# Both FFN products as seven block products for eight, in two phases, with the blocks of hid passed through DRAM

## The chip, the cores and the metric

One core of a Trainium2 chip runs the kernel in one launch. The metric is device time in microseconds. Before the change it is 3207.47 us, the median of three runs (3206.49 to 3208.62). Five engines work side by side, each through its own instructions in order: TensorE (PE), VectorE (DVE), ScalarE (ACT), GpSimd (POOL) and SyncE (SP), which here issues nearly all transfers between DRAM and the on-chip memory (SBUF). Matrix products land in a second on-chip memory, PSUM.

## The reference

The same encoder layer is applied to two batches (prompt and sample), each of 1024 rows of 1024 numbers: an input projection, two kinds of attention, a gated output projection, a layer norm, and then the feed-forward network (FFN) that the change is about. In `encoder_layer`:

```
merged = sigmoid(ga + b_gate[0]) * ya + sigmoid(gb + b_gate[1]) * yb
x = layer_norm(DEEPNORM_ALPHA * x + merged @ w_out, ln1_g, ln1_b)
hid = square(relu(x @ w_ff1 + b_ff1))          # 1024 x 4096
x = layer_norm(DEEPNORM_ALPHA * x + hid @ w_ff2 + b_ff2, ln2_g, ln2_b)
```

All of it is float32. To multiply at that accuracy, the kernel splits every operand into a high and a low part in the rounded type `fp32r`, and each product takes three matmuls: high by high, low by high, high by low (`mm3`).

## The kernel before, in words

The two batches run one after the other. In each, after attention, the output projection (`pso`, 32 sums of 24 matmuls) gives rows of `acc`; each is normalised (`layer_norm`), transposed and split into `x1T` (`transposes`), and gets its residual and bias in place (L729). High parts are casts on ScalarE; low parts are subtractions, which all go through the helper at L103, on VectorE or GpSimd.

The FFN runs over 32 slices of 128 columns of hid, two at a time (the last four together). For a slice, `wunit` (L178) loads w1's 128 columns in two tiles of 256 KB, casts them (`whi`, L189) and subtracts (`wlo`); 48 matmuls `pmm` give 1024 rows of hid in two halves; ScalarE applies bias and relu (L754), GpSimd squares (L755), ScalarE casts (L756) and VectorE subtracts, so that `hh` and `hl` stay in SBUF. A row block of w2 is loaded (512 KB, `w2r`) and split (`w2h`, `w2l`). After two slices, 16 sums `psf` of 12 matmuls each follow, and VectorE adds each to `acc` (L773). Per batch these are 1536 and 1536 matmuls. At the end each row of `acc` is normalised again and written out.

The program's order is not written out by hand: all work is emitted to a scheduler that simulates a timeline and orders the instructions of each engine. Semaphores make an engine wait for what it reads and for buffers that must come free; SP issues its transfers in order, each behind those ahead of it.

Of the kernel before, what the change touches and what calls it, by code (L numbers as in the profile page):

```python
# [9 lines left out]
F32 = mybir.dt.float32  # L10
# [71 lines left out]
def encoder_kernel(ctx, tc, xs, w_in, b_gate, w_a, w_b, w_out, rpb, ln1_g, ln1_b, w1, b1, w2, b2,  # L82
# [22 lines left out]
    def mm3(out, ah, al, bh, bl, start, stop):  # L105
        nc.tensor.matmul(out, ah, bh, start=start, stop=False)  # L106
        nc.tensor.matmul(out, al, bh, start=False, stop=False)  # L107
        nc.tensor.matmul(out, ah, bl, start=False, stop=stop)  # L108
# [15 lines left out]
    gd = [dram.tile([2, KT, P, T], F32, name=f"gd{b}") for b in range(len(xs))]  # L124
    prd = dram.tile([8, PR, PC], F32, name="prd")
# [43 lines left out]
    wup = ctx.enter_context(tc.tile_pool(name="wu", bufs=2, reuse_waits="tile"))  # L169
    wrw = ctx.enter_context(tc.tile_pool(name="wraw", bufs=3, reuse_waits="tile"))  # L170
    sm = ctx.enter_context(tc.tile_pool(name="small", bufs=8, reuse_waits="tile"))
    pmm = ctx.enter_context(tc.tile_pool(name="pmm", bufs=2, space=PSUM, reuse_waits="tile"))
# [37 lines left out]
    def layer_norm(z, g, bb, last=0, lnt=None):  # L210

        mv = sm.tile([P, 2], F32, name="mv", tag="mv")
        if last == 1:

            junk = lnt.tile([P, D], F32, name="junk", tag="x")
# [7 lines left out]
        else:  # L223
            st = sm.tile([P, 2, 6], F32, name="bst", tag="bst")
            for j in range(2):
                nc.vector.bn_stats(st[:, j], z[:, j * 512:(j + 1) * 512])
# [21 lines left out]
    for b, x in enumerate(xs):  # L248
        rop = pool("rope", side="right")
        rope = rop.tile([P, 2, T], F32, name="rope")  # L250
        maska = rop.tile([P, 512], F32, name="maska")
# [5 lines left out]
        vp = pool("v")  # L257
        vrp = pool("vr", 4)
        vtp = pool("vt", 2)
# [430 lines left out]
        abp.release()  # L690


        accp = pool("acc", side="right")
        acc = accp.tile([P, 8, D], F32, name="acc")
        lnp = pool("ln1", side="right")
        g1, bb1, b2t = bcast(lnp, ln1_g, "g1"), bcast(lnp, ln1_b, "bb1"), bcast(lnp, b2, "b2t")
        x1T = bigT()
        pso = pool("ps_o", 4, space=PSUM)
        pst = pool("ps_t2", 2, space=PSUM)
        for h in range(2):  # L700
            for nh in range(2):
                wo = []
                for k in range(KT):
# [4 lines left out]
                    nc.scalar.copy(wh, raw)  # L708
                    sub(nc.gpsimd, wl, raw, f(wh))
                    wo.append((wh, wl))  # L710
                pss = [pso.tile([P, 512], F32, name="pso", tag="pso") for _ in range(4)]
                order = [(k, i) for k in range(KT) for i in range(4)]
                if nh == 1:
                    order.sort(key=lambda o: o[1])
                for k, i in order:
                    cs = slice(i * P, (i + 1) * P)
                    mm3(pss[i], mT[h][0][:, k, cs], mT[h][1][:, k, cs], *wo[k], k == 0, k == KT - 1)
                for i in range(4):
                    it = 4 * h + i
                    xt = xp.tile([P, D], F32, name="xt", tag="x")  # L720
                    ns = slice(nh * 512, (nh + 1) * 512)
                    nc.sync.dma_start(xt[:, ns], x[it * P:(it + 1) * P, ns])
                    nc.vector.scalar_tensor_tensor(acc[:, it, ns], in0=xt[:, ns], scalar=ALPHA, in1=pss[i],
                                                   op0=ALU.mult, op1=ALU.add)
            for i in range(4):
                it = 4 * h + i
                layer_norm(acc[:, it], g1, bb1)
                transposes(acc[:, it], pst, x1T[h][0], x1T[h][1], i * P)
                nc.vector.scalar_tensor_tensor(acc[:, it], in0=acc[:, it], scalar=ALPHA, in1=b2t, op0=ALU.mult, op1=ALU.add)  # L729
        pst.release()  # L730
        pso.release()
        lnp.release()
        wop.release()


        hidp = pool("hid", 4)
        w2p = pool("w2", 4)
        w2r = pool("w2r", 2)
        tmp = pool("ffn_t", 2)
        psf = pool("ps_f", 6, space=PSUM)  # L740
        nft = FF // P
        for c in [range(i, i + 2) for i in range(0, nft - 4, 2)] + [range(nft - 4, nft)]:
            hid, w2t = [], []
            for ft in c:
                fs = slice(ft * P, (ft + 1) * P)
                wu = wunit([w1[:, fs]])
                hh = hidp.tile([P, T], F32R, name="hh", tag="hh")
                hl = hidp.tile([P, T], F32R, name="hl", tag="hl")
                for h in range(2):
                    hs = slice(512 * h, 512 * (h + 1))  # L750
# [75 lines left out]
```

## Time and profile before

| | us |
|---|---|
| median of the runs | 3207.47 |
| profiled execution | 3202.68 |
| its span, first to last instruction | 3201.0 |
| TensorE busy | 3072.3 |
| VectorE busy | 1426.0 |
| GpSimd busy | 1299.0 |
| ScalarE busy | 1143.7 |

The span is the time between the first and the last instruction of one profiled execution; the runs are timed without a profile. The FFN of the first batch lies at about 911 to 1611 us in it, that of the second at about 2490 to 3188. A matmul's recorded duration overlaps with that of the next, so the distance between starts is what counts. [...]

### The profile page before, as it was taken

The page shows a single profiled execution, that of the slowest core. Times are in us where ns is not written, and L with a number is a line of the kernel's source. Part 1 is how long each engine was busy: PE and PEld are TensorE (multiplying, and loading weights), DVE is VectorE, ACT ScalarE, POOL GpSimd, SP SyncE. Part 2 cuts the span into 40 slices and gives each one's busy share as a digit, 9 for nine tenths or more (in the row PEclk, how much of TensorE's full clock was granted, in tenths as well). Part 3 has the DMA queues.
Part 4 walks back from the last instruction along what each step waited for, and adds up shares of the span by engine and source line. Part 5 has one row for each costly group of instructions (what it writes and reads, how often), then busy time and mean ns, then how long its engine had stood idle before and what let it go on. Part 6 is the DMA issues. An engine that isn't in the chain of part 4 may idle for free. (4 is left out here: it accounts for less than half of the span.)

```text
span 3201.0 us, 39935 instructions
## 1 busy us (share of the span) xinstructions
PE 3072.3 (96%) x14732; PEld 2567.3 (80%) x14732; DVE 1426.0 (45%) x3052; ACT 1143.7 (36%) x2222; POOL 1299.0 (41%) x959
## 2 busy tenths in 40 slices
PE   8889898999999999999989989999999999999998
PEld 7778687887778888888888877778878788888886
DVE  1156556744553333333331665666446433333334
ACT  3155464654222221122331655555532321222223
POOL 3565543214643333333441647242165433333333
PEclk9999998999999999999999999999999999999999
DMA  8732324445431111111163222244454211111111
GB/s 225 254 102 71 98 63 135 124 155 164 145 96 53 53 47 53 47 40 53 61 214 106 73 66 86 87 126 142 169 163 132 73 53 46 42 52 53 50 47 53
DMA packets 306267, 309.78 MB, mean 97 GB/s; under 512 B 33992, under 2 KB 263184, under 8 KB 305816
## 3 DMA queue, kind: packets, MB, share of 16 engines
q1 hardware_dynamic: 279576, 268.95, 27.8%
q10 hardware_dynamic: 26496, 38.28, 3.3%
q8 instruction: 116, 1.90, 0.2%
q14 instruction: 79, 0.65, 0.1%
HBM read 246.02 MB, written 62.09 MB: 96 GB/s over the span
## 5 line engine op out<-in xcount | busy, mean ns | idle before, releaser
L106 PE MATMUL pmm<-bh,whi 128*128 128x512 f32 x2176 | 860.3, 395 | 17.9 <-ACT r L415 17.4
L108 PE MATMUL pmm<-bl,whi 128*128 128x512 f32 x2176 | 857.1, 394 | 0.0
L107 PE MATMUL pmm<-bh,wlo 128*128 128x512 f32 x2176 | 856.6, 394 | 0.0
L103 POOL TENSOR_TENSOR wlo<-wraw,whi 128x512 fp32r<-128x512 f32 (+1 forms) x304 | 417.2, 1389 | 518.0 <-ACT whi L189 462.8
L106 PEld LDWEIGHTS pmm<-bh,whi 128*128 128x128 f32 x2176 | 411.8, 189 | 99.3 <-ACT r L415 18.3
L108 PEld LDWEIGHTS pmm<-bl,whi 128*128 128x128 f32 x2176 | 411.4, 189 | 81.9 <-DVE bl L103 0.4
L107 PEld LDWEIGHTS pmm<-bh,wlo 128*128 128x128 f32 x2176 | 411.8, 189 | 78.9
L773 DVE TENSOR_TENSOR acc<-acc,psf 128x512 f32<-128x512 f32 x480 | 324.2, 686 | 257.5 <-PE psf L108 256.2
L103 DVE TENSOR_TENSOR hl<-r,hh 128x512 fp32r<-128x512 f32 x128 | 118.1, 923 | 636.3 <-ACT hh L756 636.1
L107 PE MATMUL psf<-w2h,hl 128*128 128x512 f32 x1024 | 398.3, 389 | 0.0
L108 PE MATMUL psf<-w2l,hh 128*128 128x512 f32 x1024 | 398.3, 389 | 0.0
L106 PE MATMUL psf<-w2h,hh 128*128 128x512 f32 x1024 | 393.0, 389 | 0.0
L103 POOL TENSOR_TENSOR w2l<-w2r,w2h 128x1024 fp32r<-128x1024 f32 x64 | 153.1, 2412 | 503.1 <-ACT w2h L763 503.1
L755 POOL TENSOR_TENSOR r<-r 128x512 f32<-128x512 f32 x128 | 134.0, 1047 | 349.2 <-ACT r L754 349.2
L763 ACT CAST w2h<-w2r 128x1024 fp32r<-128x1024 f32 x64 | 64.4, 1052 | 537.3 <-PE psf L107 532.8
L754 ACT ACTIVATE r<-pmm,b1t 128x512 f32<-128x512 f32 x128 | 88.3, 689 | 383.7 <-PE pmm L108 383.6
L108 PEld LDWEIGHTS psf<-w2l,hh 128*128 128x128 f32 x1024 | 192.3, 188 | 39.9
L107 PEld LDWEIGHTS psf<-w2h,hl 128*128 128x128 f32 x1024 | 192.2, 188 | 39.9
L106 PEld LDWEIGHTS psf<-w2h,hh 128*128 128x128 f32 x1024 | 192.2, 188 | 39.9
L355 ACT ACTIVATE smk<-smk,nm 128x256 f32<-128x256 f32 (+4 forms) x320 | 162.1, 508 | 149.7 <-DVE nm L354 145.0
L189 ACT CAST whi<-wraw 128x512 fp32r<-128x512 f32 (+1 forms) x304 | 169.8, 605 | 21.9 <-DMA wraw<-in_w_ff_dram 14.7
L103 DVE TENSOR_TENSOR ptl<-pt,pth 128x512 fp32r<-128x512 f32 (+3 forms) x224 | 125.3, 569 | 67.4 <-ACT pth L631 35.7
(144 smaller groups left out, 4717.2 us busy)
## 6 DMA issues: line engine op xcount, KB each, us to landing
wraw<-in_w_in_dram SPq DMA_DIRECT2D x144, 256.0 KB
wraw<-in_w_ff_dram SPq DMA_DIRECT2D x128, 256.0 KB
w2r<-in_w_ff_dram SPq DMA_DIRECT2D x64, 512.0 KB
gd<-gt ACTq DMA_DIRECT2D x32, 512.0 KB
sg<-gd SPq DMA_DIRECT2D x32, 512.0 KB
wor<-in_w_out_dram SPq DMA_DIRECT2D x64, 256.0 KB
vd<-vt ACTq DMA_DIRECT2D x32, 384.0 KB
bt<-bmd SPq DMA_DIRECT2D x64, 144.0 KB
```

The costliest lines, as they stand in the source:

```text
L103: eng.tensor_tensor(out, a, b, op=ALU.subtract)
L106: nc.tensor.matmul(out, ah, bh, start=start, stop=False)
L107: nc.tensor.matmul(out, al, bh, start=False, stop=False)
L108: nc.tensor.matmul(out, ah, bl, start=False, stop=stop)
L189: nc.scalar.copy(hi[:, ks], raw[:, :k])
L355: nc.scalar.activation(pr[:, e0:e1], pr[:, e0:e1], AF.Exp, bias=nm, scale=1.0, accum_out=den)
L754: nc.scalar.activation(r, ps, AF.Relu, bias=b1t[:, ft:ft + 1], scale=1.0)
L755: nc.gpsimd.tensor_tensor(r, r, r, op=ALU.mult)
L763: nc.scalar.copy(wh, raw)
L773: nc.vector.tensor_tensor(acc[:, it, ns], acc[:, it, ns], ps, op=ALU.add)
```

## The change

A product of two matrices that are cut into 2 x 2 blocks takes eight block products; with sums of blocks formed first, seven products and sums of their results do. The change does this for both FFN products.

Phase 1 computes hid. Its blocks are x1 cut at row 512 and column 512, and w1 cut at row 512 and into pairs of 128 columns. After the output projection, sums of the transposed blocks of x1 are formed (`sums1`) and split into seven operands (`blocks0`, `blocks1`); the raw blocks of the first half wait in DRAM (`rawd`), the residual rows too (`resd`). Then 16 pairs of slices follow. `job_a` makes products 1 and 2, `job_b` products 6, 5, 7, 3, 4 of a pair from `w1t` (columns of the pair's first slice), `w1b` (second slice) and the sums `ss`; a product is 12 matmuls. The first four `job_a` come ahead of all `job_b`. The blocks of hid and their sums, seven tiles `ht` or `c11` of 256 KB for each pair, are written to DRAM (`hidd`).

Phase 2 computes the rest in four chunks of four pairs. For each of the seven products of a chunk, `operands` reads two tiles of 512 KB of hid's blocks back, forms the sum of w2's blocks, and splits both; `product` runs 12 matmuls for each of four row blocks and adds the result to one or two blocks of `acc`.

Pools move as well: the pools for raw and split weights and for `pmm` are opened anew in each batch, V's tiles lie on the other side of SBUF, and `rope` is loaded after V instead of before.

The diff, cut to its core:

```diff
@@ after the output projection's operands
+        awp = pool("w1top", 2, side="right")
+        opp = pool("w1op", 3, side="right")
+        opq = pool("w1oq", 1, side="right")
...
+        def split(oh, ol, src, eng):
+            nc.scalar.copy(oh, src)
+            sub(eng, ol, src, f(oh))
+        def w1_top(p):
+            top = awp.tile([P, KT, P], F32, name="w1t", tag="w1t")
+            nc.sync.dma_start(top, w1[:, 2 * p * P:(2 * p + 1) * P].rearrange("(k p) c -> p k c", p=P))
+            return top
+        def w1_ops(src, eng):
+            oh = opp.tile([P, KT, P], F32R, name="oh", tag="oh")
+            ol = opp.tile([P, KT, P], F32R, name="ol", tag="ol")
+            split(oh, ol, src, eng)
+            return oh, ol
+        def residual(it, z):
+            zf = z.rearrange("p j c -> p (j c)")
+            nc.vector.scalar_tensor_tensor(zf, in0=zf, scalar=ALPHA, in1=b2t, op0=ALU.mult, op1=ALU.add)
+            nc.sync.dma_start(resd[b][it], zf)
+        def sums1(i, z):
+            rt = ttp.tile([P, 2, 4, P], F32, name="rt", tag="rt")
+            nc.sync.dma_start(rt, rawd[b][i])
+            pts, xr = transposed(z)
+            ta = ttp.tile([P, 4, P], F32, name="ta", tag="ta")
+            sub(nc.vector, ta, xr[:, 1], xr[:, 0])
+            sub(nc.gpsimd, rt[:, 0], xr[:, 0], rt[:, 0])
+            sub(nc.gpsimd, xr[:, 0], xr[:, 1], rt[:, 0])
+            sub(nc.gpsimd, rt[:, 1], rt[:, 1], xr[:, 0])
+            return {3: xr[:, 1], 5: rt[:, 0], 6: xr[:, 0], 7: ta, 4: rt[:, 1]}
+        def blocks1(i, z, srcs):
+            for n, m in enumerate((6, 5, 7, 3, 4)):
+                split(xb[m][0][:, :, i * P:(i + 1) * P], xb[m][1][:, :, i * P:(i + 1) * P], srcs[m], (nc.vector, nc.gpsimd)[n % 2])
+            residual(4 + i, z)
...
+        def prod(ps, w, x, start):
+            for k in range(4):
+                mm3(ps, w[0][:, k], w[1][:, k], x[0][:, k], x[1][:, k], start and k == 0, k == 3, skip=True)
+        def relu2(t):
+            nc.vector.scalar_tensor_tensor(t, in0=t, scalar=0.0, in1=t, op0=ALU.max, op1=ALU.mult)
+        def job_a(p, top):
+            o = w1_ops(top, nc.gpsimd)
+            px = psx.tile([P, 512], F32, name="px", tag="px")
+            prod(px, [t[:, :4] for t in o], xb[1], True)
+            pz = psz.tile([P, 512], F32, name="pz", tag="pz")
+            prod(pz, [t[:, 4:] for t in o], xb[2], True)
+            c11 = c11p.tile([P, 512], F32, name="c11", tag="c11")
+            nc.scalar.activation(c11, px, AF.Identity, bias=bias(2 * p), scale=1.0)
+            nc.vector.tensor_tensor(c11, c11, pz, op=ALU.add)
+            relu2(c11)
+            put(p, 1, c11)
+            return px, c11
+        early = [job_a(p, w1_top(p)) for p in range(EARLY)]
...
+        bop = pool("w1bot", 1, side="right")
+        sp_ = pool("w1s", 1, side="right")
+        pup = pool("pu", 1, side="right")
+        htp = pool("ht", 8, side="right")
+        def job_b(p, top, px, c11):
+            bot = bop.tile([P, KT, P], F32, name="w1b", tag="w1b")
+            nc.sync.dma_start(bot, w1[:, (2 * p + 1) * P:(2 * p + 2) * P].rearrange("(k p) c -> p k c", p=P))
+            ss = sp_.tile([P, 4, 4, P], F32, name="ss", tag="ss")
+            s2, s1, s3, s4 = (ss[:, i] for i in range(4))
+            a11, a12, a21, a22 = top[:, :4], top[:, 4:], bot[:, :4], bot[:, 4:]
+            nc.gpsimd.tensor_tensor(s1, a21, a22, op=ALU.add)
+            sub(nc.gpsimd, s2, s1, a11)
+            sub(nc.gpsimd, s3, a11, a21)
+            sub(nc.gpsimd, s4, a12, s2)
+            o65 = w1_ops(ss[:, 0:2].rearrange("p i k c -> p (i k) c"), nc.vector)
+            o73 = w1_ops(ss[:, 2:4].rearrange("p i k c -> p (i k) c"), nc.vector)
+            o4 = [opq.tile([P, 4, P], F32R, name=f"o4{s}", tag=f"o4{s}") for s in range(2)]
+            split(*o4, a22, nc.gpsimd)
...
+            prod(px, [t[:, :4] for t in o65], xb[6], False)
+            nc.scalar.copy(u2, px)
...
+            prod(px, o4, xb[4], False)
+            nc.scalar.activation(c21, px, AF.Identity, bias=bias(2 * p + 1), scale=1.0)
+            for t in (c12, c22, c21):
+                relu2(t)
+            put(p, 4, c22)
+            put(p, 2, c21)
+            nc.gpsimd.tensor_tensor(h1, c12, c22, op=ALU.add)
+            put(p, 5, h1)
+            sub(nc.gpsimd, h2, h1, c11)
+            put(p, 6, h2)
+            sub(nc.vector, h3, c11, c12)
+            put(p, 7, h3)
+            sub(nc.gpsimd, h4, c21, h2)
+            put(p, 3, h4)
...
+            def operands(n, m, u):
...
+                hr = hrp.tile([P, 2, 512], F32, name="hr", tag="hr")
+                nc.sync.dma_start(hr, hidd[b][p:p + 2, m - 1].rearrange("q p t -> p q t"))
...
+                split(o[:, 0], o[:, 1], hr, nc.gpsimd if n % 2 and c else nc.vector)
+                split(o[:, 2], o[:, 3], src, nc.vector if n % 2 else nc.gpsimd)
```

How the order of the engines changes is seen at two places.

TensorE at the first FFN's start, before: a transpose of the layer norm's rows (`pt`), then the FFN's first matmuls (`pmm`) at once.

```order
L107 MATMUL pso_8603<-woh_8596,bl1_7413 128x512
L108 MATMUL pso_8603<-wol_8597,bh1_7412 128x512
L205 MATMUL pt_8723<-ident_58,acc_7948 128x128 x4
L205 MATMUL pt_8730<-ident_58,acc_7948 128x128 x4
L106 MATMUL pmm_8847<-bh0_7958,whi_8835 128x512
L107 MATMUL pmm_8847<-bh0_7958,wlo_8836 128x512
L108 MATMUL pmm_8847<-bl0_7959,whi_8835 128x512
```

TensorE there after the change: the end of the early job_a's (`pz`, from `bh0`/`bl0`, x1's own blocks) and the first job_b, products 6 (`px`, with the operand `t60`) and 5 (`py`, with `t50`), which read `oh`, `ol` made from `ss`.

```order
L109 MATMUL pz_9064<-bl0_7983,oh_9047 128x512
L107 MATMUL pz_9064<-bh0_7982,oh_9047 128x512
L108 MATMUL pz_9064<-bh0_7982,ol_9048 128x512
L109 MATMUL pz_9064<-bl0_7983,oh_9047 128x512
L107 MATMUL px_8940<-t60_8830,oh_9106 128x512
L107 MATMUL py_9134<-t50_8832,oh_9106 128x512
L108 MATMUL px_8940<-t60_8830,ol_9107 128x512
L109 MATMUL px_8940<-t61_8831,oh_9106 128x512
```

Between the last row of the output projection and the row of `t60` stand 94 matmuls of the early job_a's and the last transposes; the first product that needs a sum of blocks stands behind them all.

GpSimd in the middle of the FFN, before: low parts of w1 (`wlo`) and w2 (`w2l`) and the squares (`r<-r`) of two slices.

```order
L103 TENSOR_TENSOR w2l_13042<-w2r_13039,w2h_13041 128x1024
L103 TENSOR_TENSOR w2l_13120<-w2r_13117,w2h_13119 128x1024
L755 TENSOR_TENSOR r_12848<-r_12848 128x512
L755 TENSOR_TENSOR r_12878<-r_12878 128x512
L103 TENSOR_TENSOR wlo_12968<-wraw_12969,whi_12967 128x512
L103 TENSOR_TENSOR wlo_12968<-wraw_12973,whi_12967 128x512
```

GpSimd in the middle of phase 1 after the change: one pair's sums of w1's blocks (`ss`), a low part for job_a (`ol`), the low part `o41`, and the sums of hid's blocks (`ht`).

```order
L880 TENSOR_TENSOR ss_10456<-w1b_10454 128x512 [waits DMAHW7_49]
L103 TENSOR_TENSOR ss_10456<-w1t_10417,w1b_10454 128x512
L103 TENSOR_TENSOR ss_10456<-ss_10456,w1t_10417 128x512 [waits Pool_49]
L103 TENSOR_TENSOR ss_10456<-w1t_10417,ss_10456 128x512 [waits Pool_49]
L103 TENSOR_TENSOR ol_10566<-w1t_10563,oh_10565 128x1024 [waits DMAHW2_49,Activation_49]
L907 TENSOR_TENSOR ht_10385<-ht_10382,ht_10384 128x512 [waits DMAHW5_49,DVE_49]
L103 TENSOR_TENSOR o41_10470<-w1b_10454,o40_10469 128x512 [waits PE_49,Activation_49]
L103 TENSOR_TENSOR ht_10386<-ht_10385,c11_10303 128x512 [waits DMAHW6_49,DMAHW4_49,Pool_49]
L103 TENSOR_TENSOR ht_10388<-ht_10383,ht_10386 128x512 [waits DMAHW4_49,DVE_49,Pool_49]
L880 TENSOR_TENSOR ss_10602<-w1b_10600 128x512 [waits DMAHW1_49]
```

One pair now holds nine operations. The first sum waits for the load of `w1b`; `o41`, the last reader of that buffer, waits for TensorE, which must have used the previous pair's `o41`.

SP at the same place after the change (before, it held only loads of w1 and w2 here): the writes of hid's blocks and the load of the same `w1b`.

```order
L849 DMA hidd0_76<-ht_10238 128x512 [waits DMAHW3_49,DVE_49]
L849 DMA hidd0_76<-ht_10237 128x512 [waits DMAHW4_49,DVE_49]
L849 DMA hidd0_76<-ht_10239 128x512 [waits DMAHW5_49,Pool_49]
L849 DMA hidd0_76<-ht_10241 128x512 [waits DMAHW6_49,DVE_49]
L876 DMA w1b_10454<-in_w_ff1_dram 128x8x128 [waits DMAHW7_49,Pool_49]
L849 DMA hidd0_76<-c11_10303 128x512 [waits DMAHW0_49,DVE_49]
```

The load of the next `w1b` stands behind four writes, and waits for the DMA issued eight before it (DMAHW7) and for GpSimd.

## Rows read from the trace of the kernel before

**Rows 1.** The page, part 1: busy us, share of the span, instructions.

```profile
PE 3072.3 (96%) x14732; PEld 2567.3 (80%) x14732; DVE 1426.0 (45%) x3052; ACT 1143.7 (36%) x2222; POOL 1299.0 (41%) x959
```

**Rows 2.** A stretch inside the FFN: stretch, length, busy per engine, PEclk, DMA, GB/s.

```profile
960.00:1560.00 600.00, 600.00 (x2649) 496.99 (x2648) 192.69 (x268) 133.81 (x202) 211.06 (x144) 1.00 0.17 50
```

**Rows 3.** Chain of waits, one step of the FFN loop: start, us, what.

```profile
2558.56 0.45 PE psf L106 x2
...
2602.08 0.45 PE psf L106 x2
```

**Rows 4.** Stretches of 10 us: out-projection, FFN starts, the batches' boundary.

```profile
880.00:890.00 10.00, 10.00 (x46) 8.27 (x45) 6.90 (x11) 3.46 (x7) 5.57 (x5) 1.00 0.69 201
910.00:920.00 10.00, 5.85 (x29) 4.54 (x28) 7.28 (x9) 3.83 (x7) 0.16 (x1) 0.70 0.33 105
1610.00:1620.00 10.00, 4.83 (x21) 3.59 (x21) 8.43 (x17) 5.65 (x9) 3.43 (x3) 0.69 0.77 257
1620.00:1630.00 10.00, 6.56 (x28) 4.92 (x29) 4.50 (x6) 2.39 (x6) 1.46 (x2) 0.63 0.91 303
1630.00:1640.00 10.00, 10.00 (x59) 9.24 (x58) 2.77 (x4) 4.88 (x10) 5.83 (x6) 1.00 0.92 313
2480.00:2490.00 10.00, 8.21 (x45) 6.74 (x43) 9.26 (x13) 2.15 (x4) 1.64 (x2) 1.00 0.21 58
2490.00:2500.00 10.00, 7.77 (x31) 6.13 (x32) 6.21 (x9) 4.64 (x8) 1.29 (x2) 0.66 0.14 47
```

**Rows 5.** Timeline, the last matmul: start, us, engine, line, operation.

```profile
3187.39 0.39 PE L108 MATMUL psf<-w2l,hh 128*128 128x512 f32 x1
```

**Rows 6.** Groups in 960 to 1560, shapes apart: count | busy, mean ns | idle.

```profile
L773 DVE TENSOR_TENSOR acc<-acc,psf 128x512 f32<-128x512 f32 x210 | 142.0, 686 | 112.6 <-PE psf L108 112.0
L103 POOL TENSOR_TENSOR wlo<-wraw,whi 128x512 fp32r<-128x512 f32 x58 | 86.8, 1518 | 0.0
L103 POOL TENSOR_TENSOR w2l<-w2r,w2h 128x1024 fp32r<-128x1024 f32 x28 | 66.5, 2397 | 248.9 <-ACT w2h L763 248.9
L754 ACT ACTIVATE r<-pmm,b1t 128x512 f32<-128x512 f32 x58 | 40.0, 690 | 181.8 <-PE pmm L108 181.8
L756 ACT CAST hh<-r 128x512 fp32r<-128x512 f32 x58 | 36.0, 621 | 38.4 <-POOL r L755 34.8
L763 ACT CAST w2h<-w2r 128x1024 fp32r<-128x1024 f32 x28 | 28.1, 1053 | 265.2 <-PE psf L107 265.2
```

**Rows 7.** Groups of the whole span: a GpSimd subtraction elsewhere.

```profile
L103 POOL TENSOR_TENSOR wv<-wvr,wv 128x512 fp32r<-128x512 f32 x16 | 20.3, 1290 | 44.9 <-ACT wv L272 44.9
```

**Rows 8.** Timeline 1621 to 1631: a load and its first reader.

```profile
1622.89 2.55 SPq L271 DMA_DIRECT2D wvr<-in_w_in_dram  x4
1629.96 1.04 ACT L272 CAST wv<-wvr 128x384 fp32r<-128x384 f32 x2 [3.28 <-DMA wvr<-in_w_in_dram]
```

**Rows 9.** Timeline, VectorE and GpSimd, alone and beside each other.

```profile
1102.06 1.11 DVE L103 TENSOR_TENSOR hl<-r,hh 128x512 fp32r<-128x512 f32 x1 [4.75 <-ACT hh L756]
1107.50 0.69 DVE L103 TENSOR_TENSOR hl<-r,hh 128x512 fp32r<-128x512 f32 x1 [4.33 <-ACT hh L756]
1101.33 2.98 POOL L103 TENSOR_TENSOR wlo<-wraw,whi 128x512 fp32r<-128x512 f32 x2
1605.65 3.40 DVE L237 TENSOR_TENSOR acc<-acc,bb 128x1024 f32<-128x1024 f32 x1 [1.57 <-POOL acc L236]
1609.57 1.21 DVE L237 TENSOR_TENSOR acc<-acc,bb 128x1024 f32<-128x1024 f32 x1
1603.20 4.77 POOL L236 TENSOR_TENSOR acc<-acc,g 128x1024 f32<-128x1024 f32 x2
```

**Rows 10.** Timeline at the first FFN's start: TensorE, then VectorE.

```profile
903.61 0.39 PE L108 MATMUL pso<-wol,bh 128*128 128x512 f32 x1
904.63 0.48 PE L106 MATMUL pmm<-bh,whi 128*128 128x512 f32 x1
915.05 1.23 DVE L729 SCALAR_TENSOR_TENSOR acc<-acc,b2t 128x1024 f32<-128x1024 f32 x1 [1.24 <-PE pt L205]
```

More of the change, by code (lines that the diff above doesn't have):

```diff
@@ L248, in encoder_kernel @@
     for b, x in enumerate(xs):
-        rop = pool("rope", side="right")
-        rope = rop.tile([P, 2, T], F32, name="rope")
-        maska = rop.tile([P, 512], F32, name="maska")
+        wrw = pool("wraw", 3)
+        wup = pool("wu", 2, side="right")
+        pmm = pool("pmm", 2, space=PSUM)
         xT = bigT()
@@ L315, in encoder_kernel @@
         pst.release()
+        vp.release()
         vtp.release()
         vrp.release()
-        vp.release()
+        rop = pool("rope", side="right")
+        rope = rop.tile([P, 2, T], F32, name="rope")
+        maska = rop.tile([P, 512], F32, name="maska")
         nc.sync.dma_start(rope, rope_d)
@@ L707, in encoder_kernel @@
                     wl = wop.tile([P, 512], F32R, name="wol", tag="wol")
[L708 to L709 removed]
+                    split(wh, wl, raw, nc.gpsimd)
                     wo.append((wh, wl))
                 pss = [pso.tile([P, 512], F32, name="pso", tag="pso") for _ in range(4)]
[L712 to L714 removed]
@@ new lines, in encoder_kernel @@
+            if h == 0:
+                blocks0(2, zs[2])
+                blocks0(3, zs[3])
+        wop.release()
+        wrw.release()
+        pso.release()
+        xbp = pool("xtb")
+        for m in (6, 5):
+            xb[m] = [xbp.tile([P, 4, 512], F32R, name=f"t{m}{s}", tag=f"t{m}{s}") for s in range(2)]
+        for i in range(4):
+            blocks1(i, zs[i], sums[i] if i < 2 else sums1(i, zs[i]))
+        c11p = pool("c11", 4)
+        psx = pool("ps_x", 4, space=PSUM)
+        psy = pool("ps_y", 1, space=PSUM)
@@ new lines, in encoder_kernel @@
+        for p in range(EARLY):
+            job_b(p, w1_top(p), *early[p])
+        for p in range(EARLY, NP):
+            top = w1_top(p)
+            job_b(p, top, *job_a(p, top))
+        psz.release()
+        psy.release()
+        psx.release()
+        for q in (htp, pup, sp_, bop, xap, opq, opp, awp):
+            q.release()
+        c11p.release()
+        xbp.release()
+        accp = pool("acc")
+        acc = accp.tile([P, 2, 4, 2, 512], F32, name="acc")
+        w2a = pool("w2a", 2, side="right")
```

231 lines of the change are left out of this document (154 added, 77 removed).

## The prediction

> **What bounds the kernel now.** The page's busy list comes first: TensorE is busy for 3072.3 of 3201.0 us, VectorE for 45%, GpSimd for 41% and ScalarE for 36% [rows 1]. Busy time alone decides nothing here, so I next cut out stretches by time. In 600 us in the middle of the first FFN, TensorE has no idle time at a full granted clock, while VectorE works 193, ScalarE 134 and GpSimd 211 of the 600 us and the DMA engines are at 0.17 [rows 2]. The FFN is thus bound by the number of matmuls, with room on every other engine. The chain of waits gives the price: the same step of the two-slice loop comes at 2558.56 and again at 2602.08, 43.52 us for its 192 matmuls of 128x512, so 226.7 ns each [rows 3]. (The duration of 389 ns in the groups is that of a pipelined instruction; starts are 227 ns apart.) The third view, short stretches at the edges of the FFN, shows where TensorE does wait: 4.15 us at 910 to 920, 4.0 us at 1.79 + 2.23 around 2490, each followed by work at a granted clock of 0.66 to 0.70; some 9 us of idle time between the batches at 1610 to 1630; all in [rows 4]. The tail runs from 3187.4, when the last matmul starts, to 3201.0 [rows 5].
>
> **What goes.** Each FFN matrix product of 2x2 blocks needs seven block products for eight. Counted in the order of the changed program, phase 1 has 84 matmuls per pair of slices for 96 and phase 2 336 per chunk for 384, so 16 x 12 + 4 x 48 = 384 fewer per batch, 768 in all, all 128x512. All but a few stood in stretches in which TensorE never waited, so the gross gain is 768 x 0.2267 = 174.1 us. The rest of this part is what comes back.
>
> **Phase 1, one pair.** TensorE has 84 x 0.2267 = 19.04 us of work. GpSimd gets one low part of 128x1024 (2.40 us, as w2l has it) and eight 128x512 operations: 1.29 us each where nothing disturbs them, 1.52 as wlo took them in the FFN [rows 6, 7]: 12.7 to 14.6 us. VectorE gets two low parts of 128x1024 at 1.21, and some eight operations of 128x512 at 0.69: 7.9 us. ScalarE has three casts of 1.05, one of 0.62 and five evictions of 0.69, 7.2 us, all by the nearest rows of the FFN of before [rows 6, 9]. So each engine fits, GpSimd with a fifth to a third left. DMA carries 2.75 MB in 19 us, 145 GB/s, under half of the 313 GB/s that it reached at 1630 [rows 4].
>
> What has less room is a loop of waits that before does not have. The raw lower half `w1b`, its sums `ss` and the operand `o4` have one buffer each. In the order, product 4 of a pair must end before `o41` of the next is written, that must end before the next `w1b` is loaded, and the three sums s1, s3, s2 stand behind that load on GpSimd. With t the end of product 4: cast 0.62, `o41` 1.3 to 1.5 and some queueing give t+2.8. The load: no row shows one of this size alone. Four loads of 192 KB took from 1622.89 to 1629.96 to be usable, 7.1 us with the DMA engines 0.91 busy [rows 4, 8]; 512 KB at 313 GB/s would be 1.7 us. I take 6, near the observed one, since these loads have short rows of 512 bytes too: t+9. Three sums at 1.29 to 1.52 give t+13 to 13.6; cast 1.05; VectorE's low part 1.2, and up to 2.2 more if it has to wait for GpSimd: t+15.5 to 18. TensorE reaches the next user, product 5 or 6, 85 matmuls after t, at t+19.3. So a full pair hides the loop with 1 to 4 us of slack. The SP queue puts the load behind four writes of hid; those come from VectorE and GpSimd results that are due by t+3, so I add nothing. For occasional misses I take 0.25 us a pair over 24 full pairs: **+6** (0 to 72, 3 us each).
>
> In the first four pairs of a batch job_a has been done ahead and there are only 60 matmuls, 13.6 us, to cover the loop. It needs 15.5 to 18, plus what its last part leaves: 3.5 us for each of three turns, two batches: **+21** (0 to 36).
>
> [...] At 1102.06 a VectorE subtraction took 1.11 us while two GpSimd ones stood at 2.98 for both; alone they take 0.69 and 2 x 1.29 [rows 7, 9]. At 1605.65 VectorE took 3.40 for what took 1.21 at 1609.57; it ended just after GpSimd's second multiply, 4.77 for two [rows 9]. So a late comer waits for the end of the other's operation, and each 128x512 operation costs GpSimd about 0.40. Five such VectorE operations and two of double size (0.9 each) would add 3.9 us to GpSimd's 12.7: 16.6 of 19.04.
> [...]
>
> **Start of each FFN.** Before, eight transposes and 24 matmuls follow the last `pso` (start 903.61) closely [rows 10]. Now 94 matmuls of job_a are left for it, 21.3 us, which with the transposes reach to T0+23 (T0 is the end of the last `pso`). But product 6 needs `w1b`, whose place in memory is free only after the last residual. Before, VectorE started its last residual at 915.05, 11 us after T0, behind a late transpose [rows 10]. After, four rows of blocks are split there as well: 4 x (three low parts of 0.69 and one residual of 1.2) = 13 us, of which some lies before that transpose, so T0+20; load 6, T0+26; three sums that stand behind the GpSimd part of those blocks, T0+31 to 33; cast, T0+34. TensorE then idles 11 us or more, up to 21 if GpSimd pays the port at every operation, where it idled 4.15: +7 to +17. I take **+11**, two batches: **+22**. Out-projection: residuals and raw blocks add 8 MB in its 384 x 0.2267 = 87 us, 94 GB/s on top of the up to 201 of its stretches, still under what 1630 reached [rows 4]; +2.5 each for single late tiles, **+5** (-4 to 10).
>
> **Phase 2.** Products take 48 matmuls, 10.9 us; an operand pair needs two reads of 512 KB, four casts of 1.05 and four low parts of 1.2 or 2.4, 8 us on the busiest engine. A chunk is 76.2 us of TensorE against some 43 of GpSimd and 54 of VectorE. It fits, less well than before in the FFN. The switch from phase 1 waits for the last writes of hid: **+3.5** for both batches. In chunk 0 both low parts of hid fall to VectorE and the accumulations also wait for the residual reads, so PSUM comes free late: +4.5 each, **+9** (0 to 30). Chunks 1 to 3: 1.5 each, **+9** (0 to 24).
>
> **Edges.** The boundary: pools for weights open anew per batch, V moves to the other side, and rope is loaded later; first `psv` comes at much the same place, **+1.5** (-4 to 10). Tail: two more accumulations, **+2**. [...]
>
> Sum: 6 + 21 + 22 + 5 + 3.5 + 9 + 9 + 1.5 + 2 + 2 = 81 us back. The profiled execution took 3202.68 us (1.7 around its span), so 3202.68 - 174.1 + 81 = 3109.6. It was 4.8 us below the median of the runs, 3207.47, and I add that: **3114 us**.
>
> **Rivals.** (A) All of it hides: only the FFN start (16) and the tail (2) return, as the FFN of before never waited [rows 2]. 3207.5 - 174.1 + 18 = 3051; with half of the early loop 3062. Against it: the loop is longer than 13.6 us by its own rows. 14%.
> [...] If a VectorE operation holds off GpSimd for its whole duration, GpSimd's 12.7 and VectorE's 5.9 us of two-input work (5 x 0.69 + 2 x 1.21) make 18.6 of 19.04; no slack is left to make up a late load, and the sums and low parts in the loop each wait 0.7 to 1.2 us for one another, five times. The loop then takes 20.5 to 22 us, about 2 more a pair: 24 x 2 - 6 = +42, so 3156 us. For it: the 3.40 us at 1605.65, and that GpSimd worked only 211 of 600 us in the FFN so far [rows 2], so that no row shows it near full. [...] 18%.
> (C) Slower. The single-buffered `w1b` is a round trip of DMA, GpSimd, ScalarE, VectorE and TensorE, run 32 times. With 99 us of gain left without its own term (174 - 75), it eats all of it at 24 x 4.1 us, a loop of 23.4 us. That needs a load of 9 us rather than 6 (its issue behind late writes on SP) and GpSimd sums of 2.2 rather than 1.4. At 25 us: 24 x 5.7 - 6 = +131, so 3245 us. Against it: DMA is less than half loaded. 8%.
> That the matmuls are not saved is out: they are counted.
>
> **How the numbers follow.** Forecast 60% (3080 to 3145), A 14%, B 18%, C 8%. For 8 in 10, I leave out half of A, C and the end of B: 3058 to 3185. About 6 us (0.2%) is what a measurement can tell from no change. Faster: forecast, A, B and a little of C (below 23.4 us of loop), 0.90; within 0.2% 0.02; slower 0.08.
>
> **What would show it.** Steady phase 1 with starts of like products 19.0 to 19.3 us apart and TensorE busy over 97%; the early pairs 16 to 18 us apart instead of 13.6, with TensorE waiting for `oh`; one hole of 11 to 21 us at the FFN start in each batch, and phase 2 chunks of 76 to 78 us, the first 80. A steady pair of 20.5 us or more, with GpSimd above 90%, shows B; a wait for `w1b` in every pair shows C. No hole at the start and early pairs of 13.6 us would show A.

## The result and the profile after

The changed kernel takes 3224.89 us (median of five runs, 3217.89 to 3226.86) against 3207.47: a ratio of 1.0053, 95% interval 1.0035 to 1.007. It is slower by half a per cent, where 3114 us and a range up to 3185 were forecast. The profiled execution took 3217.89 us, its span 3216.1.

The page, part 1, of the changed kernel:

```profile
PE 2971.4 (92%) x13964; PEld 2446.1 (76%) x13964; DVE 1888.6 (59%) x3192; ACT 1301.9 (40%) x2342; POOL 1735.1 (54%) x1099
```

Against [rows 1], TensorE has 768 matmuls fewer and is busy 101 us less, but VectorE is busy 463 and GpSimd 436 us more. The stages, from the starts of matmuls in both traces, first and second batch:

| stage | before, us | after, us |
|---|---|---|
| first `psv` to first `pso` | 804.2, 756.2 | 815.3, 768.8 |
| output projection | 92.2, 90.6 | 94.8, 93.8 |
| FFN, last `pso` to last matmul | 706.9, 706.8 | 702.6, 704.7 |
| last matmul of the first batch to first `psv` | 23.3 | 13.2 |
| tail | 13.6 | 15.4 |

The FFN should have lost 87 us a batch and lost 2 to 4. Inside it, after: the first product with a sum starts 49.4 and 49.2 us after the last `pso`; from there to the end of the fourth `job_b` pass 69.3 and 72.0 us, for 262 matmuls (59.4 us at 226.7 ns), so 17.3 and 18.0 for each early pair; the other 985 matmuls of phase 1 take 233.9 and 236.2 (223.3 at 226.7 ns); the switch to phase 2 4.9 and 4.2; the four chunks 91.8, 84.5, 81.9, 87.0 and 90.3, 84.1, 81.9, 86.9, where 336 matmuls are 76.2. Job_a runs ahead of job_b by a changing distance, so a steady pair is measured between starts of product 6 that lie eight pairs (672 matmuls) apart: 20.12 and 20.19 us.

What TensorE waits for, whole span (engine, line, what it waited for: us, times, longest):

```profile
PE px L107 <- DVE acc L998: 30.9, 9, 6.3
PE pz L107 <- DVE c L860: 29.5, 6, 9.0
PE pmm L107 <- ACT r L420: 24.7, 2, 18.5
PE px L107 <- ACT oh L719: 16.2, 5, 4.7
PE px L108 <- DVE bh L103: 15.2, 2, 7.9
```

Only the `pmm` wait has a counterpart before. The largest two are waits for additions on VectorE, which lie behind its low parts. Stretches (as in [rows 4]; PEclk is the granted clock as a share of the full one): the FFN's start, steady phase 1, and the end of a chunk:

```profile
917.60:969.60 52.00, 31.84 (x124) 24.09 (x123) 48.88 (x40) 19.26 (x33) 47.30 (x27) 0.82 0.40 126
1040.00:1260.00 220.00, 216.18 (x927) 173.41 (x926) 114.55 (x110) 73.18 (x101) 160.01 (x101) 1.00 0.45 145
1418.00:1440.00 22.00, 15.66 (x67) 12.63 (x66) 18.77 (x11) 7.78 (x8) 21.41 (x7) 0.89 0.27 82
```

At the start VectorE and GpSimd are both busy over 90% (48.9 and 47.3 of 52 us), and at the chunk's end for 85 and 97% (18.8 and 21.4 of 22). In between, phase 1 runs with TensorE at 98% and GpSimd at 73% (160 of 220); but 927 matmuls in 220 us are 237 ns each, so a busy TensorE is not at its pace of 227 ns there. The timeline at those two places, VectorE's rows and then GpSimd's:

```profile
942.34 1.78 DVE L103 TENSOR_TENSOR ta<-xr 128x512 f32<-128x512 f32 x1
944.05 1.78 DVE L103 TENSOR_TENSOR t<-xr,t 128x512 fp32r<-128x512 f32 x1
945.75 1.75 DVE L103 TENSOR_TENSOR t<-ta,t 128x512 fp32r<-128x512 f32 x1
943.53 1.75 POOL L103 TENSOR_TENSOR rt<-xr,rt 128x512 f32<-128x512 f32 x1
945.24 1.72 POOL L103 TENSOR_TENSOR bl<-xr,bh 128x512 fp32r<-128x512 f32 x1
...
1421.23 3.24 DVE L103 TENSOR_TENSOR ts<-rw,rw 128x1024 f32<-128x1024 f32 x1 [3.54 <-DMA rw<-in_w_ff_dram]
1427.73 3.42 DVE L103 TENSOR_TENSOR rw<-rw,rw 128x1024 f32<-128x1024 f32 x1
1431.08 3.40 DVE L103 TENSOR_TENSOR bh<-hr,bh 128x1024 fp32r<-128x1024 f32 x1
1423.35 3.38 POOL L103 TENSOR_TENSOR rw<-rw,rw 128x1024 f32<-128x1024 f32 x1
1426.69 3.38 POOL L103 TENSOR_TENSOR bh<-rw,bh 128x1024 fp32r<-128x1024 f32 x1
1430.03 3.37 POOL L103 TENSOR_TENSOR bl<-rw,bl 128x1024 fp32r<-128x1024 f32 x1
```

A 128x512 subtraction takes 1.75 us on VectorE and 1.72 on GpSimd, where [rows 7, 9] have 0.69 and 1.29; one of 128x1024 takes 3.4 on either, where they have 1.21 and [rows 6] 2.40. From start to start it is 1.69 and 3.36 us, near the sum of both engines' times alone (1.98 and 3.61): each step of one engine now lasts about as long as one step of both together, they take turns. All these operations have both inputs in SBUF.

### The profile page after: what moved, and what is told of

Read it like the earlier page. It is cut to its first block, busy times and chain, and to the rows that moved or that the text cites. A ratio compares the mean times of both kernels' runs of the same rounds, so it can differ in the third digit from the quotient of the medians.

```text
span 3216.1 us, 39721 instructions
## 1 busy us (share of the span) xinstructions
PE 2971.4 (92%) x13964; PEld 2446.1 (76%) x13964; DVE 1888.6 (59%) x3192; ACT 1301.9 (40%) x2342; POOL 1735.1 (54%) x1099
## 3 DMA queue, kind: packets, MB, share of 16 engines
q1 hardware_dynamic: 364696, 415.78, 40.6%
## 5 line engine op out<-in xcount | busy, mean ns | idle before, releaser
L103 POOL TENSOR_TENSOR wlo<-wraw,whi 128x512 fp32r<-128x512 f32 (+1 forms) x176 | 228.2, 1310 | 526.1 <-ACT whi L190 457.6
L107 PE MATMUL pmm<-bh,whi 128*128 128x512 f32 x1152 | 466.5, 405 | 25.5 <-ACT r L420 24.7
L108 PE MATMUL pmm<-bh,wlo 128*128 128x512 f32 x1152 | 463.5, 402 | 0.0
L109 PE MATMUL pmm<-bl,whi 128*128 128x512 f32 x1152 | 463.5, 402 | 0.0
L107 PEld LDWEIGHTS pmm<-bh,whi 128*128 128x128 f32 x1152 | 220.7, 192 | 69.9 <-ACT r L420 25.6
L109 PEld LDWEIGHTS pmm<-bl,whi 128*128 128x128 f32 x1152 | 220.3, 191 | 44.9
L108 PEld LDWEIGHTS pmm<-bh,wlo 128*128 128x128 f32 x1152 | 220.6, 191 | 42.3
L107 PE MATMUL px<-bh 128*128 128x512 f32 x256 | 104.0, 415 | 45.3 <-DVE acc L998 30.9
L107 PE MATMUL psv<-wv,bh 128*128 128x384 f32 (+1 forms) x384 | 139.9, 366 | 5.6 <-DVE vt L103 4.5
L108 PE MATMUL psv<-wv,bl 128*128 128x384 f32 (+1 forms) x384 | 139.2, 364 | 0.0
L109 PE MATMUL psv<-wv,bh 128*128 128x384 f32 (+1 forms) x384 | 138.2, 362 | 0.2 <-POOL wv L103 0.2
L108 PE MATMUL px<-bh 128*128 128x512 f32 x256 | 104.1, 413 | 15.2 <-DVE bh L103 15.2
```

The costliest lines, as they stand in the source:

```text
L103: eng.tensor_tensor(out, a, b, op=ALU.subtract)
L107: nc.tensor.matmul(out, ah, bh, start=start, stop=False, skip_group_check=skip)
L108: nc.tensor.matmul(out, al, bh, start=False, stop=False, skip_group_check=skip)
L109: nc.tensor.matmul(out, ah, bl, start=False, stop=stop, skip_group_check=skip)
```

## The experiments

Where no interval is given, the time is that of a single run. Five runs of the changed kernel spread over 9 us, so smaller differences are read from the stages in the traces and not from the time.

**Holding off or slow?** Two kernels on phase 2. The first (e4_phase2_dve) moves all its sums and low parts to VectorE:

```diff
-                eng = (nc.gpsimd, nc.vector)[u]
+                eng = nc.vector
-                split(o[:, 0], o[:, 1], hr, nc.gpsimd if n % 2 and c else nc.vector)
-                split(o[:, 2], o[:, 3], src, nc.vector if n % 2 else nc.gpsimd)
+                split(o[:, 0], o[:, 1], hr, nc.vector)
+                split(o[:, 2], o[:, 3], src, nc.vector)
```

> The changed kernel with every low part and every sum of w2's blocks in phase 2 on VectorE, none on GpSimd. Theory (holding off): at a chunk's end the two engines now take 3.35 us for one operation of each of 128x1024, against 1.21 alone on VectorE; so VectorE does all of it in no more time than now, 66 us of a chunk's 76, the idle time at chunk ends (6.3 and 3.9 us, px waiting for acc) shrinks by half or more, 10 to 25 us less in all. Rival (VectorE's queue is the bound): it delays the accumulations further, chunks of 80 to 85 us, 15 to 40 us more.

Measured: 3155.04 us, 70 less than the changed kernel's median, though VectorE was given more work. Chunks took 81.2, 76.2, 76.2, 76.0 and 80.8, 76.2, 76.2, 78.6 us. The theory had the direction and expected a third of the gain. That GpSimd holds VectorE off and that GpSimd is slower by itself would both give such a gain. The second (e8_phase2_idle_work) tells them apart and adds idle work back, in a tile that is never read:

```diff
+                for _ in range(2 if m in (6, 7) else 1):
+                    sub(nc.gpsimd, dum, g2, bb2)
```

> The kernel of e4_phase2_dve (phase 2's sums and low parts all on VectorE) with 18 GpSimd subtractions of 128x1024 per chunk added, on constant tiles and into a tile that nobody reads: as many as were moved away, but nothing waits for them. Theory (the two engines hold each other off): VectorE's operations of two SBUF inputs go back from 1.2 to 2 us or more beside them, and phase 2 loses a large part of the 70 us that the move gained: 3185 us or more. Rival (GpSimd was merely slow, 2.4 us against 1.2, and on the path): nobody waits for these, so 3150 to 3162 us as without them.

Measured: 3338.06 us, 183 more than without, for work that nobody waits for. In the first batch chunks of 114.0, 116.6 and 91.4 us while it lasts, then 76.0. The groups of phase 2 (1290 to 1490 us, shapes apart) in the changed kernel, then with all on VectorE, then with the idle work:

```profile
L103 DVE TENSOR_TENSOR bh<-hr,bh 128x1024 fp32r<-128x1024 f32 x12 | 23.4, 1953 | 7.2 <-ACT bh L719 7.2
L998 DVE TENSOR_TENSOR acc<-acc,px 128x512 f32<-128x512 f32 x28 | 18.6, 679 | 8.4 <-PE px L109 8.4
L103 POOL TENSOR_TENSOR bl<-rw,bl 128x1024 fp32r<-128x1024 f32 x7 | 23.7, 3385 | 0.0
L103 POOL TENSOR_TENSOR bh<-hr,bh 128x1024 fp32r<-128x1024 f32 x5 | 12.1, 2411 | 27.3 <-ACT bh L719 27.3
```

```profile
L103 DVE TENSOR_TENSOR bh<-hr,bh 128x1024 fp32r<-128x1024 f32 x19 | 23.2, 1222 | 16.0 <-ACT bh L719 16.0
L998 DVE TENSOR_TENSOR acc<-acc,px 128x512 f32<-128x512 f32 x28 | 18.9, 679 | 6.0 <-PE px L109 6.0
```

```profile
L103 DVE TENSOR_TENSOR bl<-hr,bl 128x1024 fp32r<-128x1024 f32 x12 | 37.5, 3122 | 0.0
L103 DVE TENSOR_TENSOR bh<-hr,bh 128x1024 fp32r<-128x1024 f32 x12 | 28.2, 2353 | 0.0
L1001 DVE TENSOR_TENSOR acc<-acc,px 128x512 f32<-128x512 f32 x12 | 8.0, 674 | 0.0
L103 POOL TENSOR_TENSOR dum<-g,bb 128x1024 f32<-128x1024 f32 x56 | 181.1, 3234 | 29.2 <-DMA bb<-in_ln_b_dram 24.9
```

The same low part on VectorE (`bh<-hr,bh`) is 1953 ns beside GpSimd, 1222 without and 2353 beside the idle work (3122 for the one into `bl`); GpSimd's own low parts are 2411 to 3385. The addition `acc<-acc,px`, with one input in PSUM, stays at 674 to 679 ns in all three. So it is shown that the two engines hold each other off, with two inputs in SBUF, and that this alone can lengthen a chunk, since nobody waited for the idle work. The 183 us are not the price in the changed kernel: here VectorE does all 36 operations of a chunk instead of 18, and GpSimd, with nothing to wait for, runs the idle work of four chunks within the first three. How much of the 70 us was GpSimd's own slowness, 2.4 us against 1.2, is not separated.

**The start of the FFN.** First the sums and low parts of x1's blocks on VectorE (e3_start_dve):

```diff
-            sub(nc.gpsimd, rt[:, 0], xr[:, 0], rt[:, 0])
-            sub(nc.gpsimd, xr[:, 0], xr[:, 1], rt[:, 0])
-            sub(nc.gpsimd, rt[:, 1], rt[:, 1], xr[:, 0])
+            sub(nc.vector, ...)                      # all three
-                split(..., srcs[m], (nc.vector, nc.gpsimd)[n % 2])
+                split(..., srcs[m], nc.vector)
```

> The changed kernel with the sums of x1's blocks and all low parts of its second half on VectorE instead of half of them on GpSimd (20 operations of 128x512 per batch moved). Theory (VectorE and GpSimd hold each other off at the start of the FFN: 1.75 us for what takes 0.69 alone on VectorE, 1.72 for 1.29 on GpSimd): the first product with a sum starts 8 to 12 us earlier after the last output projection matmul than the 49 us it now takes, so 15 to 20 us less in all, about 3205 us. Rival (the start hangs on the load of w1b behind the last residual, and on the one PSUM bank of pz): VectorE gets more work, the residual comes later, 0 to 10 us more.

Measured: 3212.83 us; the first product with a sum at 45.6 and 44.4 instead of 49.4 and 49.2 us, half of what was expected. The direction is the theory's, the size is not, and the trace shows why. The waits for the first `w1b` and the third sum of blocks, in the changed kernel and then in this one:

```profile
957.01 1.30 POOL L880 TENSOR_TENSOR ss<-w1b 128x512 f32<-128x512 f32 x1 [1.15 <-DMA w1b<-in_w_ff_dram]
964.10 1.71 POOL L103 TENSOR_TENSOR ss<-ss,w1t 128x512 f32<-128x512 f32 x1
```

```profile
949.21 0.47 SPq L876 DMA_DIRECT2D w1b<-in_w_ff_dram  x1
955.31 1.27 POOL L880 TENSOR_TENSOR ss<-w1b 128x512 f32<-128x512 f32 x1 [12.89 <-DMA w1b<-in_w_ff_dram]
959.43 1.26 POOL L103 TENSOR_TENSOR ss<-ss,w1t 128x512 f32<-128x512 f32 x1
```

With GpSimd relieved, it stands idle for 12.89 us until `w1b` has landed, 6 us after a load that SP issues 33 us after the last `pso`, right behind the last residual's write. So here the rival's load is what sets the start.

Then the place and queue of the first `w1b` (e10_w1b_free_after):

```diff
-        g1, bb1, b2t = bcast(lnp, ln1_g, "g1"), bcast(lnp, ln1_b, "bb1"), bcast(lnp, b2, "b2t")
+        b2t, g1, bb1 = bcast(lnp, b2, "b2t"), bcast(lnp, ln1_g, "g1"), bcast(lnp, ln1_b, "bb1")
-            nc.sync.dma_start(bot, ...)
+            (nc.scalar if p == 0 else nc.sync).dma_start(bot, ...)
```

> The same two edits on the changed kernel itself, where the blocks' sums and low parts are spread over VectorE and GpSimd and the first w1b is issued 34 us after the last output projection matmul. Theory (load's place sets the start): the first product with a sum at 40 to 44 instead of 49 us, 10 to 18 us less in all. Rival (the two engines, both over 90% busy there and holding each other off, set it): still 47 us or later, under 5 us less.

Measured: 3224.43 us, and the product still at 49.2 us in both batches. The load was issued 29.5 us after the last `pso` instead of 34, but of the sums behind it the third, which the first product needs, came at 46 us as before. The load on ScalarE's queue, then GpSimd's sums, in the timeline of this run:

```profile
945.95 0.42 ACTq L876 DMA_DIRECT2D w1b<-in_w_ff_dram  x1
...
954.75 1.73 POOL L880 TENSOR_TENSOR ss<-w1b 128x512 f32<-128x512 f32 x1
956.43 1.73 POOL L103 TENSOR_TENSOR ss<-w1t,w1b 128x512 f32<-128x512 f32 x1
962.74 1.77 POOL L103 TENSOR_TENSOR ss<-ss,w1t 128x512 f32<-128x512 f32 x1
966.15 2.26 POOL L103 TENSOR_TENSOR ss<-w1t,ss 128x512 f32<-128x512 f32 x1
```

Between the second and the third sum GpSimd had other work in its queue, and each takes 1.7 us or more. The rival holds for the changed kernel: its load could come 4.7 us earlier and the product no earlier, since GpSimd has other work in front of the third sum. What a load at 20 us would do is not shown: it was issued only at 29.5, behind casts in ScalarE's queue.

**All of the FFN on VectorE** (e5_ffn_dve). The edits of e3 and e4, and in `job_a` and `job_b` every `nc.gpsimd` replaced by `nc.vector`.

> The changed kernel with all sums and low parts of the FFN (start, phase 1 and phase 2) on VectorE, none on GpSimd. Theory (what costs time is that GpSimd and VectorE hold each other off): VectorE alone needs 14.6 us of a pair's 19.04, the sums of a pair take 0.69 instead of 1.3 to 1.7 us each, so the early pairs go from 17.3 to 14 to 15 us, the first product with a sum from 49 to about 42 us after the output projection, and phase 2 chunks stay at 76.2: 3095 to 3125 us. Rival (VectorE becomes the bound in phase 1, in-order behind evictions): pairs of 20 us or more, early pairs no faster, 3150 us or more.

Measured: 3124.05 us. First product with a sum at 40.6 and 41.8, as the theory had it; early pairs 16.1 and 17.1 instead of 14 to 15; steady pairs, start to start, 19.53; chunks as in e4. VectorE, busy for about 167 of the 220 us from 1040 to 1260, does not become the bound.

**The pace of matmuls.** In the changed kernel matmuls of 512 columns start 226.7 ns apart in phase 2 but 232 to 233 in most of phase 1 and in attention's projections. Sorted by the addresses that the program gives their two SBUF operands, the slower ones are those whose start addresses differ by 128 modulo 256 bytes. One longer constant shifts the lower side (e1_offset):

```diff
-    mhalf = const.tile([P, 1], F32, name="mhalf")
+    mhalfp = const.tile([P, 33], F32, name="mhalf")
+    mhalf = mhalfp[:, 0:1]
```

> The changed kernel with one constant tile made 128 bytes longer, so that every tile on the lower side of SBUF starts 128 bytes later; no instruction is added. In the trace of the changed kernel, matmuls of 512 columns start 226.7 to 228 ns apart where the two operands' start addresses agree modulo 256 bytes, and 232 to 233 ns apart where they differ by 128 bytes: attention's pmm, V's psv, and six of seven products of phase 1. Theory (relative offset sets the pace): all of these go to 227 ns, 5040 matmuls times 5.5 to 6 ns and psv, so about 35 us less, 3185 to 3195 us, and the order of the engines is as it was. Rival (the pace is slower because the operands lie far apart, or because of the DMA writes of phase 1): 232 to 233 ns remain and the time is 3218 to 3227 us.

Measured: 3217.74 us (ten runs), ratio to before 1.0027 (1.0017 to 1.0036). Groups of the whole span, changed kernel, then this one:

```profile
L109 PE MATMUL py<-bl,oh 128*128 128x512 f32 x128 | 50.6, 395 | 0.0
L108 PE MATMUL pz<-bh,ol 128*128 128x512 f32 x128 | 53.2, 416 | 0.0
```

```profile
L109 PE MATMUL py<-bl,oh 128*128 128x512 f32 x128 | 49.8, 389 | 0.0
L108 PE MATMUL pz<-bh,ol 128*128 128x512 f32 x128 | 52.9, 413 | 0.0
```

The matmuls of phase 1 did get faster (`py` 395 to 389 ns; starts 227.0 ns apart), but steady pairs took 20.05 us instead of 20.12 and 20.19: the time went into waits. The mechanism was right and the forecast of 35 us was wrong, it gave 7, less than the spread between single runs. The same offset put into the kernel before (e2_before_offset):

```diff
+    padp = ctx.enter_context(tc.tile_pool(name="padl", bufs=1, reuse_waits="tile"))
+    padt = padp.tile([P, 32], F32, name="padt")
+    nc.gpsimd.memset(padt, 0.0)
     wup = ctx.enter_context(tc.tile_pool(name="wu", bufs=2, reuse_waits="tile"))
```

> The kernel before with an unused tile of 128 bytes between the transposed x and all tiles above it on the lower side, so that the weights of the input projection, of V, of FFN1 and of the output projection differ by 128 bytes from x. Theory (relative offset): pmm, psv and pso go from 227 to 232.5 ns, psf stays at 226.7 and py, whose operands lie on either side, falls from 232.4 to 227: 8000 matmuls times 5.5 ns, 35 to 45 us more, about 3245 us. Rival: no change, 3200 to 3212 us.

Measured: 3247.11 us, 39 above the median of before. The last 190 `pmm` of the FFN in its timeline, first and last:

```profile
3144.21 0.40 PE L108 MATMUL pmm<-bl,whi 128*128 128x512 f32 x1
3188.31 0.39 PE L108 MATMUL pmm<-bl,whi 128*128 128x512 f32 x1
```

44.10 us for 189 steps, 233.3 ns each; before it was 226.7 there. `psf`, both of whose operands moved, stayed at 227.0, and `py`, whose operands lay 128 bytes apart before and no longer do, fell from 232.4 to 227.1.

**Rope.** SP's row and GpSimd's in the changed kernel's timeline show a wait of 7.58 us for `rope`, which SP now issues only at 168.6 (the edit below is e6_rope_early):

```profile
168.60 0.43 SPq L324 DMA_DIRECT2D rope<-in_rope_dram  x1
176.39 1.29 POOL L422 TENSOR_TENSOR r<-r,rope 128x512 f32<-128x512 f32 x1 [7.58 <-DMA rope<-in_rope_dram]
```

```diff
+        rop = pool("rope", side="right")     # and its two loads, moved up here
         vrp = pool("vr", 4, side="right")
```

> The changed kernel with rope and maska opened and loaded before V's pools, as in the kernel before. In the trace of the changed kernel GpSimd waits 7.6 us for rope at 176 us and the first score product comes at 203 instead of 188 us; the output projection starts 11 to 12 us later after V's start than before in both batches. Theory (the late rope is the cause): the output projection starts at 811 to 815 instead of 822.7 us, and likewise in the second batch, 12 to 22 us less in all. Rival (the slower pace of the projection's matmuls, 232.4 instead of 227.8 ns, is the cause): under 4 us less.

Measured: 3223.61 us, no gain in the end. The first batch's output projection starts at 813.1 instead of 822.7, as the theory had it, but its FFN took 707.3 us instead of 702.6 and the boundary 17.4 instead of 13.2, for reasons that are not shown; the second batch takes 770.6 us from `psv` to `pso`, not less. Late rope explains the first batch; what delays the second by 12 us is only in part the pace of `pmm` (with the longer tile it took 766.3 against 768.8, where before it was 756.2), the rest stays open.

**Together** (e7_all). e5 with rope early and the longer tile:

> The kernel of e5_ffn_dve with rope loaded before V and with the constant tile made 128 bytes longer, so that operands on the two sides of SBUF agree modulo 256 bytes. Theory: gains add where TensorE is now the bound: another 12 to 20 us from rope and 15 to 30 us from the pace of pmm, psv and phase 1 (pairs of 19.05 us), 3060 to 3090 us, 4 to 5% under the kernel before. Rival (the loops of waits hold the pace, as when only the tile was lengthened): 3095 us or more.

Measured: 3101.64 us, ratio to before 0.9679 (0.9661 to 0.9698), 3.2% faster than the kernel before, but 22 us under e5 where 27 to 50 were expected. The time lies in the rival's range, though not for its reason: steady pairs take 19.04 us from start to start, the pace of 84 matmuls at 226.7 ns. The FFNs take 641.3 and 645.4 us. Its page, part 1, and a stretch of its phase 1 (TensorE without a pause, GpSimd without work):

```profile
PE 2917.0 (94%) x13964; PEld 2433.7 (79%) x13964; DVE 1948.2 (63%) x3652; ACT 1306.1 (42%) x2342; POOL 836.0 (27%) x639
...
1030.00:1220.00 190.00, 190.00 (x840) 157.33 (x839) 136.09 (x191) 66.12 (x90) 0.00 (x0) 1.00 0.47 153
```

Against the page of the changed kernel, GpSimd is busy 899 us less and VectorE only 60 more; TensorE is busy 54 us less, in part by the better pace. The longer tile alone, taken out again (e11_all_but_offset):

> The kernel of e7_all without the longer constant tile, so with the operands of attention's pmm, of psv and of most of phase 1 again 128 bytes apart modulo 256. Lengthening the tile gained 7 us of 35 on the changed kernel, where loops of waits held phase 1 at the same pace. Theory (it counts where TensorE is the bound): pairs of phase 1 go from 18.66 to 19.1 us and pmm from 228.6 to 232.4 ns, so 12 to 22 us more than e7_all, 3112 to 3124 us. Rival (the offset never matters for the end): within 4 us of 3101.6.

Measured: 3120.86 us, ratio 0.9733 (0.9716 to 0.9751): 19 us for 128 bytes, steady pairs of 19.53 us instead of 19.04. In phase 1, where TensorE is now the bound, the pace counts in full; on the changed kernel, where loops of waits set the pairs, it hardly did. Last, the two edits on the first `w1b` once more, on e7 (e9_w1b_free):

> The kernel of e7_all with the three rows of the first layer norm laid out in another order in SBUF, so that the first w1b no longer takes the place of b2t (which the last residual reads) but of bb1 (which the last layer norm reads), and with this first load issued from ScalarE's queue, since on SP's it stands behind the write of the last residual. In e7_all it is issued 31 us after the last output projection matmul, 0.4 us after the last residual's write, and the first product with a sum starts at 42 to 43 us. Theory (this load's place and queue set the start, as the prediction had it): issued at 20 to 25 us, the first such product at 34 to 38 us, 8 to 16 us less in all, 3085 to 3094 us. Rival (VectorE, busy 48 of the first 52 us, sets the start whenever w1b lands): within 3 us of e7_all's 3101.6.

Measured: 3101.24 us, the same; the product at 41.9 and 42.0. But the load was issued at 29.7 us, behind casts in ScalarE's queue, and not at 20 to 25, so the theory was hardly tested. That VectorE sets the start here is argued from its 48 busy us of 52: its first sum follows the work before it without a pause.

## Why the prediction was wrong

The gross gain was right: 768 matmuls went, at 226.7 ns. What came back was not 81 us but about 189. By its own terms, both batches together in us, rounded, the measured ones from the profiled execution against the kernel before:

| term | forecast | measured |
|---|---|---|
| start of the FFN | 22 | 35 |
| early pairs, with the clock | 21 + 2 | 22 |
| other pairs of phase 1 | 6 | 23 |
| switch, chunk 0, chunks 1 to 3 | 3.5, 9, 9 | 9, 30, 49 |
| output projection, tail | 5, 2 | 6, 2 |
| boundary | 1.5 | -10 |
| V to output projection | nothing | 24 |

- **The step that failed** is "It fits, less well than before in the FFN", on phase 2. It looked at GpSimd's 43 and VectorE's 54 us of a chunk's 76 each for itself, as if the two ran side by side. (The 54 do not come out of the order: 18 operations at 1.21 and 32 additions at 0.69 are 44.) They take turns on operations with two SBUF inputs (128x1024 at a chunk's end: 3.4 us on either, 1.21 and 2.40 alone). Even the sum of these over a chunk, 43 and 22, is under 76; but the work comes in bunches, and at a chunk's end 7 operations on each, which alone take 16.8 and 8.5 us, take 22 on either, while TensorE waits up to 6.3 us for the additions that stand behind them. Taking GpSimd out of phase 2 gave 70 us back, and idle work put on it, for which nothing waited, cost 183; so that the sharing costs time there is shown. The price was at hand: the prediction worked the sharing out for phase 1 alone, from [rows 9], and in rival B, where a VectorE operation holds GpSimd off for its whole duration.
- **The start**: the first product was due at 34 and came at 49 us. In the prediction's chain the last residual was due at 20 and ended at 34; the load then took 5.2 us (6 were taken), the three sums and the cast 10 (8 were taken). VectorE's 27 operations from T0 to that residual would take 21 us at the durations that they have alone, an estimate from rows of e3 and of the changed kernel; so 20 would have been about right had nothing held VectorE off, and what failed is again the sharing. The 11 us a batch in the sum come from a range whose upper end has GpSimd pay for a port; no run shows a port. What the runs show there is a 128x512 operation of 1.75 us on VectorE and 1.72 on GpSimd beside each other, for 0.69 and 1.29 alone. That the load sets the start, as the prediction had it, holds in e3; in the changed kernel the two engines' queues are as long (e10), and with all of it on VectorE the load lands less than 1 us after VectorE is ready for it (e5, e7).
- **Early and steady pairs**: early pairs 17.3 and 18.0 us, in the 16 to 18 named, though each holds 65 matmuls instead of 60. Steady pairs 20.12 and 20.19, over the 19.0 to 19.3 named and nearer to rival B's 20.5, though GpSimd was busy for 73% there and not for B's 90%. Of the 1.1 us over 19.04, 0.5 is the matmuls' pace with operands 128 bytes apart (19.53 in e11, without GpSimd), which the prediction did not have; the rest were waits, and they went with GpSimd's work (e5). C's 23.4 did not come. The four loads from which the 6 us were taken have rows of 1536 bytes, not 512, and no run shows what the length of the rows does to a load; the first `w1b` took 5.2. The sum's last 2 us, for the clock, no run shows as a time of their own; what the traces show is a mean granted clock of 0.82 over the 52 us of the start above, and 0.70 at 910 to 920 before [rows 4].
- **Costed at nothing**: what the pools' move does to attention. The later rope was named, but priced only for the first `psv`; with the 128 bytes it was among the causes of 11 and 13 us between V and the output projection. Rope explains the first batch, the second stays open for the most part. The order of SP and the tiles' addresses would have shown that both moved.
- The boundary is a gain nobody counted: V's first matmuls follow the last chunk more closely.
- The rivals: B named what decided, that the two engines hold each other off, with the wrong place. That each engine's share is below one, on which the chance of 60% rests, does not mean that there is slack where work comes in bunches.

## What to carry to other kernels

VectorE and GpSimd behaved here as one engine for operations that read two SBUF operands (128x1024: 3.4 us on either beside the other): add their times before asking whether they fit, stretch by stretch, and prefer VectorE, which here took half of GpSimd's time for the same tile (1.22 us against 2.40). When work per matmul grows, as it does with fewer and more elaborate products, put that sum beside TensorE's time in the narrowest stretch, not over the whole span. And check where a change of pools puts operands and loads: here it moved addresses and a table that no line of the new algorithm mentions.

## What the hardware showed that was not expected

A matmul of 512 columns in this type started 226.7 to 228 ns after the one before it when its two SBUF operands' start addresses agreed modulo 256 bytes, and 232 to 234 ns when they differed by 128, in both kernels, whether both lay on one side of SBUF or on either side; 128 bytes of padding moved it both ways (e1, e2, e11 against e7), worth 7, 19 and 39 us here. The addresses are those of the program's layout. In the changed kernel `pso`, 256 or 768 bytes apart modulo 1024, started every 227.1 ns, and attention's `pmm`, 384 or 896 apart, every 233.0, both means over all 512-column steps without a pause. Other differences than 0 and 128 modulo 256 did not occur in the two kernels, so how it goes between them is open, and so is its cause.
